# Routing pieces tied behind the one-hots, half-tile staging and fourteen leading up products, in a two-block transformer kernel

## The chip, the cores and the metric

The kernel runs on one core of a Trainium2 chip, as one launch. The metric is the device time of one execution in microseconds (us), as the median of repeated runs. The profile is of one execution; its times count from the first instruction of the span.

## The reference, cut to what matters

Two transformer blocks run over 512 tokens of width 1024, in float32. The change touches only the last layer of the second block, a mixture of 16384 tiny experts. For each token, `experts` are found as pairs of keys: eight heads, 16 pairs each, so 128 experts per token, each with a gate.

```python
def block(args):
    xb, eb, gb = args
    ub = u[eb]
    vb = v[eb]
    act = jax.nn.gelu(jnp.einsum('cd,ced->ce', xb, ub), approximate=False) * gb
    return jnp.einsum('ce,ced->cd', act, vb)
```

## The kernel before, in words

All large products run on TensorE (PE) as three fp32r products of split operands: `pump` loads a weight tile `w` (128x1024, 512 KB) by SyncE's DMA queue, ScalarE (ACT) rounds it to `wh`, and VectorE (DVE) or GpSimd (POOL) subtracts to get `wl`. The list `lsplit` says whose turn it is. Three slots each of `w`, `wh` and `wl` let loads run three tiles ahead of the splits, and splits three ahead of the products.

The expert layer (`peer`) treats tokens in four groups of 128. Group 0 gathers its experts' rows by indirect DMA. Groups 1 to 3 (384 tokens) work densely: for each of the 128 first keys j, `up(j)` multiplies the 384 tokens with 128 experts (24 matmuls of 384 columns, called one up product here), the result passes GELU, is multiplied by a gate matrix for j, and goes through the down product into six PSUM tiles. 42 of the 128 up products (`NA`) are made early: `up_store` writes their GELU to DRAM (`Hd`). They fill TensorE while the gate matrices are made, in the stage that this change is about:

- `route(t)` finds the 16 best pairs for each head of group t: eight `top16` searches, some twenty small operations on 128x128 tiles, and twice three operations on 128x2048 elements, all on VectorE, with one Exp on ScalarE. `transposed(t)` turns its three results by TensorE into the tile `rt`.
- `onehots(t, rt)` makes the gate matrices. It takes four tokens at a time, 32 times (a "quad", `q4`): `oh1` compares the first key with 0 to 127 (on POOL for a third of the quads, else on VectorE), `oh2` the second key, times the gate. A third of the quads scale `oh2` on ScalarE, the others make it by four VectorE instructions. Four fp32 matmuls of oh1 and oh2 (two records each in the trace) give 4x128x128 gates in PSUM, and ScalarE copies them into `stage`, two tiles that hold 64 of the columns j for all 128 tokens each. `fill(1)` places one up product after every fifth quad.
- For groups 1 and 2 both tiles then go to DRAM (`Gd`), in eight DMAs of 1 MB in rows of 512 bytes (the flush), with two up products after each pair. Group 3 stays in `stage`.

A scheduler orders the instructions of each engine ahead of time; on the chip every engine and every DMA queue then runs in that order. VectorE's tables of 0 to 127 and 0 to 15 lie in PSUM (`iotp`, `iotap`).

Of the kernel before, what the change touches and what calls it, by code (L numbers as in the profile page):

```python
# [43 lines left out]
def body(tc, A, out, upto=None, dbg=None):  # L44
# [13 lines left out]
    def mmps():  # L58
        return psum.tile([P, 512], F32, name="mm", tag="mm", bufs=4)
# [1094 lines left out]
    def peer(norm):  # L1154
# [95 lines left out]
                if ahead:  # L1250
                    up_store(ahead.popleft())

        def route(t):
            V.tensor_copy(tfp.rearrange("p (a b) -> p a b", b=16), ti[t])
            tf = tfp.rearrange("p (h f k) -> p h f k", f=2, k=16)


            bv = r_("bv", (P, 8, 16))
            bi = r_("bi", (P, 8, 16), dt=U32)
            cd = r_("cd", (P, 8, 60))  # L1260
            lists = tv[t].rearrange("p (h f) k -> p h f k", f=2)
            for i0, n, w, o in ((0, 1, 16, 0), (1, 2, 8, 16), (3, 5, 4, 32), (8, 8, 1, 52)):
                V.tensor_tensor(cd[:, :, o:o + n * w].rearrange("p h (i j) -> p h i j", j=w),
                                lists[:, :, 0, i0:i0 + n].rearrange("p h (i o) -> p h i o", o=1)
                                .to_broadcast([P, 8, n, w]),
                                lists[:, :, 1, 0:w].rearrange("p h (o j) -> p h o j", o=1)
                                .to_broadcast([P, 8, n, w]), ALU.add)
            for h in range(8):
                top16(bv[:, h], bi[:, h], cd[:, h])
            pf = r_("pf", (P, 8, 16))  # L1270
            V.tensor_copy(pf, bi)
            fi, fj, w_ = (r_(n, (P, 8, 16)) for n in ("fi", "fj", "fw"))
            for n, (sh, off) in enumerate(((3, -1.0), (2, -5.0))):
                pi = r_("pi", (P, 8, 16), dt=U32)
                V.tensor_scalar(pi, bi, sh, None, op0=ALU.logical_shift_right)
                V.tensor_copy(w_, pi)
                if n == 0:
                    V.tensor_scalar(fi, w_, off, 0.0, op0=ALU.add, op1=ALU.max)
                else:
                    V.scalar_tensor_tensor(fi, w_, off, fi, op0=ALU.add, op1=ALU.max)  # L1280
            V.scalar_tensor_tensor(fi, pf, -44.0, fi, op0=ALU.add, op1=ALU.max)
            V.scalar_tensor_tensor(fj, fi, -16.0, pf, op0=ALU.mult, op1=ALU.add)
            for m, off in ((-8.0, -8.0), (-4.0, -20.0), (-1.0, -44.0)):
                V.scalar_tensor_tensor(w_, fi, m, pf, op0=ALU.mult, op1=ALU.add)
                V.scalar_tensor_tensor(fj, w_, off, fj, op0=ALU.add, op1=ALU.max)
# [12 lines left out]
            gt = gate0 if t == 0 else r_("gt", (P, P), bufs=2)
# [7 lines left out]
            return ev[0], ev[1], gt  # L1306


        stp = rctx.enter_context(tc.tile_pool(name="st", bufs=1, side="right", reuse_waits="tile"))
        def transposed(t):  # L1310
            pt = axps()
            for n, a in enumerate(route(t)):
                PE.transpose(pt[:, n * P:(n + 1) * P], a, ident)
            rt = b_("rt", (P, 3, P), bufs=3)
            SC.activation(rt, pt[:, :3 * P].rearrange("p (n k) -> p n k", n=3), AF.Copy)
            return rt

        def onehots(t, rt):
            io4 = iotp.rearrange("p (o i) -> p o i", o=1).to_broadcast([P, 4, P])
            stage = [stp.tile([P, 64, P], F32, name="stage", tag="stage", bufs=2) for _ in range(2)]  # L1320
            for q4 in range(32):
                t4 = slice(4 * q4, 4 * q4 + 4)

                def cols(n):
                    return rt[:, n, t4].rearrange("p (t o) -> p t o", o=1).to_broadcast([P, 4, P])
                oh1 = b_("oh1", (P, 4, P), bufs=3)
                if q4 % 3 == 1:
                    for k in range(4):
                        G.tensor_scalar(oh1[:, k], iot, rt[:, 0, 4 * q4 + k:4 * q4 + k + 1], None, op0=ALU.is_equal)
                else:  # L1330
                    V.tensor_tensor(oh1, cols(0), io4, ALU.is_equal)
                oh2 = b_("oh2", (P, 4, P), bufs=3)
                on_act = q4 % 3 == 0
                if on_act:
                    V.tensor_tensor(oh2, cols(1), io4, ALU.is_equal)
                pg = axps()
                for k in range(4):
                    tk = 4 * q4 + k
                    if on_act:
                        SC.activation(oh2[:, k], oh2[:, k], AF.Copy, scale=rt[:, 2, tk:tk + 1])  # L1340
                    else:
                        V.tensor_scalar(oh2[:, k], iotp, rt[:, 1, tk:tk + 1], rt[:, 2, tk:tk + 1],  # L1342
                                        op0=ALU.is_equal, op1=ALU.mult)
                    PE.matmul(pg[:, k * P:(k + 1) * P], lhsT=oh1[:, k], rhs=oh2[:, k], start=True, stop=True)  # L1344
                for jh in range(2):
                    SC.activation(stage[jh][:, :, t4].rearrange("p j t -> p t j"),  # L1346
                                  pg.rearrange("p (t j) -> p t j", t=4)[:, :, jh * 64:jh * 64 + 64], AF.Copy)
                if q4 % 5 == 2:
                    fill(1)
            if t == 3:  # L1350
                return stage
            lsplit[:] = [V, G]
            for n in range(4):
                for j0 in (0, 16):
                    jj = 32 * (n % 2) + j0
                    nc.sync.dma_start(Gd[64 * (n // 2) + jj:64 * (n // 2) + jj + 16, :, (t - 1) * P:t * P]
                                      .rearrange("j i t -> i j t"), stage[n // 2][:, jj:jj + 16])
                fill(FLUSH[n])

        lsplit[:] = [V, G]  # L1360
        fill(FIRST)
        for t in (1, 2, 3):
            rt = transposed(t)
            lsplit[:] = [G]
            stage = onehots(t, rt)
        fill(NA)
        e1, e2, _ = route(0)
        V.scalar_tensor_tensor(e1, e1, 128.0, e2, op0=ALU.mult, op1=ALU.add)
        V.tensor_copy(idx, e1)
        lctx.close()  # L1370
# [84 lines left out]
            fetched[j] = gm, g  # L1455

        def gate(j):
            gm, st = fetched.pop(j)
            g = (mmps, axps)[turn[0] % 2]()[:, :TD]
            turn[0] += 1  # L1460
            if st is None:
                up(j, g)
                SC.activation(g, g, AF.Gelu)
            else:
                SC.activation(g, st, AF.Copy)
            V.tensor_tensor(g[:, :2 * P], g[:, :2 * P], gm, ALU.mult)
            V.tensor_tensor(g[:, 2 * P:], g[:, 2 * P:], stage[j // 64][:, j % 64], ALU.mult)
            a = hp.tile([P, TD], F32R, name="ah", tag="ah", bufs=3)
            b = hp.tile([P, TD], F32R, name="al", tag="al", bufs=3)
            SC.activation(a, g, AF.Copy)  # L1470
            last_dve[0] = V.tensor_tensor(b, g, a.bitcast(F32), ALU.subtract)  # L1471
            waiting.append((j, a, b))
# [219 lines left out]
```

## Time and profile before

| | us |
|---|---|
| median of three runs | 2961.1 (2959.9 to 2962.53) |
| the profiled execution, its own time | 2960.28 |
| its span, first to last instruction | 2957.9 |
| busy in the span: PE, DVE, ACT, POOL | 2900.9, 1929.8, 1376.7, 1158.4 |

The profiled execution lies 0.8 us below the median, and 2.4 us of its time lie outside the span. TensorE is busy for 98% of the span, VectorE for 65%. The one-hot stage begins with the first matmul on `xnh` at 1750.02 us and ends with the transposes of L1404 at 2054.66 us. A matmul's record is longer than its turn on the engine, since records overlap; a turn is read from starts that follow each other.

### The profile page before, as it was taken

The numbers are of one execution on the slowest core, as the hardware profiler recorded it, in microseconds if no ns is written. First come the engines' busy times: TensorE is split into PE (matmuls) and PEld (weight loads), VectorE is DVE, ScalarE is ACT, GpSimd is POOL, SyncE is SP. The second block draws the span as 40 slices with busy tenths as digits, with TensorE's granted clock in tenths as the row PEclk, the third lists the DMA queues.
The fourth block names the chain that finished last, engine by engine and source line by source line (L and its number), as shares of the span: only waits on it lengthen the run. The fifth ranks groups of instructions, "written<-read, shape, count | busy, mean of one in ns | idle before, by whom it ended". The sixth has DMA issues, their size and how long they took to land.

```text
span 2957.9 us, 46911 instructions
## 1 busy us (share of the span) xinstructions
PE 2900.9 (98%) x18211; PEld 2619.5 (89%) x18211; DVE 1929.8 (65%) x3505; ACT 1376.7 (47%) x2346; POOL 1158.4 (39%) x749
## 2 busy tenths in 40 slices
PE   8999999999999999999999999889999999999998
PEld 8999999988899999776688888888889888888887
DVE  4556645567664646537655788888677776776676
ACT  4454433356542425434544447567444444444444
POOL 4224323342232424104421435446455554555453
PEclk9999999999999999999999999999999999999999
DMA  4112333331123223221142232773888888888885
GB/s 136 67 52 101 98 96 101 97 104 36 65 97 97 96 98 110 85 72 52 49 150 66 86 111 79 226 225 113 304 330 311 312 317 316 330 307 302 308 315 188
DMA packets 166126, 473.41 MB, mean 160 GB/s; under 512 B 15368, under 2 KB 79240, under 8 KB 149520
## 3 DMA queue, kind: packets, MB, share of 16 engines
q1 hardware_dynamic: 135840, 322.73, 32.4%
q0 software_dynamic: 18432, 134.23, 11.8%
q10 hardware_dynamic: 11632, 13.46, 1.4%
q8 instruction: 143, 2.34, 0.3%
q14 instruction: 79, 0.65, 0.1%
HBM read 443.23 MB, written 27.13 MB: 159 GB/s over the span
## 4 chain that ended last, share of the span: by engine, by line
PE 89%; DVE 4%; ACT 3%; DMA 2%; issue 2%; POOL 1%; SPq 0%; ACTq 0%; DVEq 0%; POOLq 0%
PE mm L192 65%; PE ax L192 16%; PE ax L1344 2%; DMA w<-in_pu_dram 1%; ACT wh L115 1%; ACT stage L1346 1%; PE mm L1027 1%; PE ax L478 1%; PE ax L1207 1%; PE ax L997 0%; PE ax L453 0%; DVE wl L118 0%; DVE oh L1342 0%; PE mm L1021 0%; DMA xT<-in_xT_dram 0%
## 5 line engine op out<-in xcount | busy, mean ns | idle before, releaser
L118 POOL TENSOR_TENSOR wl<-w,wh 128x1024 fp32r<-128x1024 f32 x242 | 618.5, 2556 | 1058.2 <-ACT wh L115 893.7
L115 ACT ACTIVATE wh<-w 128x1024 fp32r<-128x1024 f32 (+1 forms) x530 | 560.0, 1057 | 854.1 <-PE mm L192 484.9
L192 PE MATMUL mm<-sh,wh 128*128 128x256 f32 (+2 forms) x3144 | 747.7, 303 | 7.0 <-ACT sh L225 6.2
L192 PE MATMUL mm<-sl,wh 128*128 128x256 f32 (+2 forms) x3144 | 744.6, 302 | 1.8 <-POOL sl L205 1.6
L192 PE MATMUL mm<-sh,wl 128*128 128x256 f32 (+2 forms) x3144 | 743.1, 301 | 1.0 <-DVE wl L118 1.0
L118 DVE TENSOR_TENSOR wl<-w,wh 128x1024 fp32r<-128x1024 f32 (+1 forms) x288 | 367.9, 1277 | 284.1 <-ACT wh L115 275.7
L192 PEld LDWEIGHTS mm<-sh,wh 128*128 128x128 f32 (+1 forms) x3144 | 498.9, 188 | 40.1 <-ACT sh L225 6.2
L192 PEld LDWEIGHTS mm<-sl,wh 128*128 128x128 f32 (+1 forms) x3144 | 497.9, 188 | 31.8 <-POOL sl L205 2.0
L192 PEld LDWEIGHTS mm<-sh,wl 128*128 128x128 f32 (+1 forms) x3144 | 497.9, 188 | 30.1 <-DVE wl L118 1.3
L192 PE MATMUL mm<-xnh,wl 128*128 128x384 f32 x688 | 237.1, 345 | 4.5 <-POOL wl L118 3.9
L192 PE MATMUL mm<-xnh,wh 128*128 128x384 f32 x688 | 237.5, 345 | 4.0 <-ACT wh L115 3.9
L192 PE MATMUL mm<-xnl,wh 128*128 128x384 f32 x688 | 236.8, 344 | 0.0
L285 DVE TENSOR_TENSOR xT<-xT,mm 128x512 f32<-128x512 f32 x80 | 54.7, 686 | 163.4 <-PE mm L192 163.4
L192 PE MATMUL mm<-wh,al 128*128 128x512 f32 x384 | 150.1, 391 | 2.5 <-DVE al L1471 2.5
L192 PE MATMUL mm<-wh,ah 128*128 128x512 f32 x384 | 150.3, 391 | 1.7 <-ACT ah L1470 1.7
L192 PE MATMUL mm<-wl,ah 128*128 128x512 f32 x384 | 150.2, 391 | 0.0
L192 PE MATMUL ax<-wh,ah 128*128 128x512 f32 x384 | 149.8, 390 | 0.0
L192 PE MATMUL ax<-wl,ah 128*128 128x512 f32 x384 | 149.7, 390 | 0.0
L192 PE MATMUL ax<-wh,al 128*128 128x512 f32 x384 | 149.4, 389 | 0.0
L561 POOL TENSOR_TENSOR y<-y 128x512 f32<-128x512 f32 x44 | 56.9, 1293 | 220.7 <-ACT y L560 220.7
L553 DVE SCALAR_TENSOR_TENSOR y<-u,vecs,y 128x512 f32<-128x512 f32 x88 | 113.9, 1295 | 44.5 <-ACT y L552 44.5
L192 PEld LDWEIGHTS mm<-xnh,wh 128*128 128x128 f32 x688 | 131.3, 191 | 6.4 <-ACT wh L115 4.6
(465 smaller groups left out, 5434.7 us busy)
## 6 DMA issues: line engine op xcount, KB each, us to landing
w<-in_pu_dram SPq DMA_DIRECT2D x128, 512.0 KB
w<-in_pv_dram SPq DMA_DIRECT2D x128, 512.0 KB
w<-in_up_dram SPq DMA_DIRECT2D x88, 512.0 KB
w<-in_down_dram SPq DMA_DIRECT2D x48, 512.0 KB
Gd<-stage SPq DMA_DIRECT2D x16, 1024.0 KB
gm<-Gd SPq DMA_DIRECT2D x128, 128.0 KB
w<-in_pq_dram SPq DMA_DIRECT2D x16, 512.0 KB
Hd<-gel ACTq DMA_DIRECT2D x42, 192.0 KB
```

The source lines that it names most:

```text
L115: SC.activation(h[:, :n], w[:, :n], AF.Copy)
L118: ins = eng.tensor_tensor(l[:, :n], w[:, :n], h[:, :n].bitcast(F32), ALU.subtract)
L192: PE.matmul(ps[:, c:c + w], lhsT=a, rhs=b[:, c:c + w], start=start and c == 0 and a is lh and b is rh, stop=stop and c + w == n and a is ll)
L285: V.tensor_tensor(xT[:, c], xT[:, c], ps, ALU.add)
L478: PE.matmul(ps[:, s], lhsT=a, rhs=b, start=i == 0, stop=i == len(mms) - 1)
L553: V.scalar_tensor_tensor(y, u[:, 0:S], w[0], y, op0=ALU.mult, op1=ALU.add)
L561: G.tensor_tensor(val, val, gate, ALU.mult)
L1027: PE.matmul(po[e * 64:e * 64 + 64, c * P:], lhsT=vs[:, c, hd * 64:hd * 64 + 64], rhs=at[:, c * P:], start=c == 0, stop=c == 3)
L1207: PE.matmul(pss[:, t * P:(t + 1) * P], lhsT=q[:, t * P:(t + 1) * P], rhs=sk, start=True, stop=True)
L1344: PE.matmul(pg[:, k * P:(k + 1) * P], lhsT=oh1[:, k], rhs=oh2[:, k], start=True, stop=True)
L1346: SC.activation(stage[jh][:, :, t4].rearrange("p j t -> p t j"), pg.rearrange("p (t j) -> p t j", t=4)[:, :, jh * 64:jh * 64 + 64], AF.Copy)
```

## The change

The routing of the next group no longer stands between two groups. `route` becomes a generator that stops after each piece; `onehots(t, rt, nxt)` runs the next group's pieces behind its own quads, where `issue_after` ties each piece on VectorE behind the instruction `own` of that quad. The yielded costs set how many pieces follow a quad. `oh2` is now scaled on ScalarE for every second quad; the other quads make it by two VectorE instructions on 128x512 elements, by way of a PSUM tile of the pool that the up products use. A stage tile now holds all 128 columns for 64 tokens; one ScalarE copy of 128x512 takes the place of two of 128x256, and each half is flushed when its 16 quads are done, in eight DMAs of 512 KB in rows of 256 bytes. Fourteen up products in place of six stand ahead of the first routing, two follow every seven quads, none stands with the flush, and all weight splits of the stage are POOL's. In the later stage each gate multiply reads two 64-column pieces of `stage` in place of one of 128.

```diff
-FIRST, FLUSH = 6, (2, 2, 2, 2)
+FIRST = 14
...
-        def route(t):
+        def route(t, out):
...
+            yield 1.5
             for h in range(8):
                 top16(bv[:, h], bi[:, h], cd[:, h])
+                yield 1.3
...
-        def onehots(t, rt):
+        def onehots(t, rt, nxt):
...
-            stage = [stp.tile([P, 64, P], F32, name="stage", tag="stage", bufs=2) for _ in range(2)]
+            res, spent, nrt = [], 0.0, None
+            steps = route(nxt, res)
+            stage = []
             for q4 in range(32):
+                if q4 % 16 == 0:
+                    st = stp.tile([P, P, 64], F32, name="stage", tag="stage", bufs=2)
+                    stage.append(st)
...
-                on_act = q4 % 3 == 0
-                if on_act:
-                    V.tensor_tensor(oh2, cols(1), io4, ALU.is_equal)
+                if q4 % 2 == 0:
+                    own = V.tensor_tensor(oh2, cols(1), io4, ALU.is_equal)
+                    for k in range(4):
+                        SC.activation(oh2[:, k], oh2[:, k], AF.Copy, scale=rt[:, 2, 4 * q4 + k:4 * q4 + k + 1])
+                else:
+                    eq = mmps().rearrange("p (t j) -> p t j", t=4)
+                    V.tensor_tensor(eq, cols(1), io4, ALU.is_equal)
+                    own = V.tensor_tensor(oh2, eq, cols(2), ALU.mult)
...
-                        V.tensor_scalar(oh2[:, k], iotp, rt[:, 1, tk:tk + 1], rt[:, 2, tk:tk + 1],
-                                        op0=ALU.is_equal, op1=ALU.mult)
...
+                SC.activation(st[:, :, o:o + 4].rearrange("p j t -> p t j"),
+                              pg.rearrange("p (t j) -> p t j", t=4), AF.Copy)
+                while spent < 1.45 * (q4 + 1) and steps is not None:
+                    with tc.issue_after(own.ins):
+                        c = next(steps, None)
...
-                if q4 % 5 == 2:
+                if q4 % 7 in (2, 5):
                     fill(1)
-            lsplit[:] = [V, G]
-            for n in range(4):
...
-                fill(FLUSH[n])
+                if q4 % 16 == 15 and t < 3:
+                    c0 = (t - 1) * P + (q4 // 16) * 64
+                    for j0 in range(0, P, 16):
+                        nc.sync.dma_start(Gd[j0:j0 + 16, :, c0:c0 + 64].rearrange("j i t -> i j t"),
+                                          st[:, j0:j0 + 16])
...
-        lsplit[:] = [V, G]
+        lsplit[:] = [G]
         fill(FIRST)
...
-            V.tensor_tensor(g[:, 2 * P:], g[:, 2 * P:], stage[j // 64][:, j % 64], ALU.mult)
+            for n, st in enumerate(stage):
+                c = slice(2 * P + n * 64, 2 * P + n * 64 + 64)
+                V.tensor_tensor(g[:, c], g[:, c], st[:, j], ALU.mult)
```

On VectorE, before the change, the routing of group 2 runs in one stretch between the one-hots of groups 1 and 2 (L1284 and L1285 are small steps, L1290, L1293 and L1296 the wide ones, L118 a weight split):

```order
L1290 TENSOR_TENSOR oh<-fi,ax 128x2048
L1285 SCALAR_TENSOR_TENSOR fj<-fw,fj 128x128
L1293 TENSOR_TENSOR oh<-oh,ax 128x2048
L118 TENSOR_TENSOR wl<-w,wh 128x1024
L1284 SCALAR_TENSOR_TENSOR fw<-fi,pf 128x128
L1296 TENSOR_REDUCE e_19175<-oh 128x128
```

On VectorE with the change, at the same steps of that routing (now L1295, L1288, L1289, L1299 and L1303), one-hots of group 1 stand between (L1346 is `oh1`, L1349 the compare of an even quad, L1354 and L1355 the two instructions of an odd one):

```order
L1295 TENSOR_TENSOR oh<-fi,ax 128x2048
L1289 SCALAR_TENSOR_TENSOR fj<-fw,fj 128x128
L1346 TENSOR_TENSOR oh_18738<-rt,ax 128x512
L1288 SCALAR_TENSOR_TENSOR fw<-fi,pf 128x128
L1349 TENSOR_TENSOR oh_18740<-rt,ax 128x512
L1289 SCALAR_TENSOR_TENSOR fj<-fw,fj 128x128
L1354 TENSOR_TENSOR mm<-rt,ax 128x512
L1288 SCALAR_TENSOR_TENSOR fw<-fi,pf 128x128
L1355 TENSOR_TENSOR oh_18791<-mm,rt 128x512
L1289 SCALAR_TENSOR_TENSOR fj<-fw,fj 128x128
L1299 TENSOR_TENSOR oh<-oh,ax 128x2048
```

The routing pieces moved between the one-hots, and the weight split left VectorE; the last routing piece of a group stands at quad 22 or 23 of 32, and only one-hots follow.

On SyncE's DMA queue, before the change, weight loads (L110) stand between the pairs of the flush (L1356):

```order
L1356 DMA Gd<-stage 128x16x128 x2
L110 DMA w<-in_pu_dram 128x1024
L1356 DMA Gd<-stage 128x16x128 x2
L110 DMA w<-in_pu_dram 128x1024 x2
L1356 DMA Gd<-stage 128x16x128 x2
L110 DMA w<-in_pu_dram 128x1024 x2
L1356 DMA Gd<-stage 128x16x128 x2
L110 DMA w<-in_pu_dram 128x1024 x9
```

On the same queue with the change, each half tile's flush (L1376) is one block of eight, in both groups:

```order
L110 DMA w<-in_pu_dram 128x1024 x16
L1376 DMA Gd<-stage 128x16x64 x8
L110 DMA w<-in_pu_dram 128x1024 x4
L1376 DMA Gd<-stage 128x16x64 x8
L110 DMA w<-in_pu_dram 128x1024 x5
L1376 DMA Gd<-stage 128x16x64 x8
L110 DMA w<-in_pu_dram 128x1024 x4
L1376 DMA Gd<-stage 128x16x64 x8
L110 DMA w<-in_pu_dram 128x1024 x3
```

The flush moved from two places to four, and the weight loads stand behind whole blocks of eight. In ScalarE's order the rounding of that weight stands 11 or 12 quads after the copy that starts the flush.

## Rows read from the trace of the kernel before

**Rows 1.** Windows: busy us per engine, granted clock, DMA share, GB/s.
```profile
core 0: us, PE busy (x) PEld busy (x) DVE busy (x) ACT busy (x) POOL busy (x), PEclk, DMA share, GB/s
1750.00:2055.00 305.00, 281.56 (x1799) 270.44 (x1798) 263.98 (x775) 205.24 (x428) 154.03 (x163) 0.96 0.50 157
1776.00:1792.00 16.00, 10.12 (x51) 9.92 (x50) 15.30 (x30) 2.98 (x5) 4.76 (x2) 0.79 0.27 102
1792.00:1850.00 58.00, 56.81 (x406) 54.21 (x404) 48.30 (x118) 51.31 (x119) 37.53 (x49) 1.00 0.20 67
1850.00:1890.00 40.00, 34.15 (x179) 32.65 (x178) 34.05 (x106) 14.23 (x23) 8.33 (x8) 0.87 1.03 307
2075.00:2945.00 870.00, 868.26 (x4296) 776.43 (x4295) 627.50 (x871) 382.81 (x729) 453.42 (x228) 1.00 0.83 305
```

**Rows 2.** Waits of PE, 1750 to 2055 us: total, times, longest.
```profile
PE ax L1344 <- ACT oh L1340: 7.6, 10, 4.3
PE ax L1313 <- DVE e L1296: 5.9, 1, 5.9
```

**Rows 3.** The chain that ended last, in order of time: start, us, what.
```profile
1799.63 1.90 PE ax L1344 x16
2049.97 4.69 PE mm L192 x27
2054.66 0.87 PE ax L1404 x8
```

**Rows 4.** Timeline of PE: start, us, engine, line, operation.
```profile
1750.02 0.33 PE L192 MATMUL mm<-xnh,wh 128*128 128x384 f32 x1
...
1791.59 0.27 PE L1313 MATMUL ax<-ident,gt 128*128 128x128 f32 x1
...
1794.25 2.05 PE L1344 MATMUL ax<-oh,oh 128*128 128x128 f32 x16
```

**Rows 5.** Timeline of DVE, 1757 to 1800 us.
```profile
1758.15 0.41 DVE L1254 CAST ax<-ti 128x256 f32<-128x256 uint32 x1
...
1759.60 0.35 DVE L1185 MAX8 bv<-cd 128x8 f32<-128x60 f32 x2
...
1762.30 1.21 DVE L118 TENSOR_TENSOR wl<-w,wh 128x1024 fp32r<-128x1024 f32 x1
...
1767.40 0.27 DVE L1300 TENSOR_TENSOR gt<-bv 128x128 f32<-128x128 f32 x1
...
1773.63 2.50 DVE L1285 SCALAR_TENSOR_TENSOR fj<-fw,fj 128x128 f32<-128x128 f32 x1
1776.05 2.27 DVE L1293 TENSOR_TENSOR oh<-oh,ax 128x2048 f32<-128x2048 f32 x1
...
1781.85 0.28 DVE L1285 SCALAR_TENSOR_TENSOR fj<-fw,fj 128x128 f32<-128x128 f32 x1
...
1792.42 0.69 DVE L1331 TENSOR_TENSOR oh<-rt,ax 128x512 f32<-128x512 f32 x1 [1.12 <-ACT rt L1315]
1793.02 0.68 DVE L1335 TENSOR_TENSOR oh<-rt,ax 128x512 f32<-128x512 f32 x1
1793.62 1.36 DVE L1342 TENSOR_SCALAR oh<-ax,rt 128x128 f32<-128x128 f32 x4
1794.90 0.68 DVE L1331 TENSOR_TENSOR oh<-rt,ax 128x512 f32<-128x512 f32 x1
```

**Rows 6.** Timeline of POOL, 1772 to 1784 us.
```profile
1773.03 2.95 POOL L118 TENSOR_TENSOR wl<-w,wh 128x1024 fp32r<-128x1024 f32 x1 [5.91 <-ACT wh L115]
```

**Rows 7.** Timeline of ACT, 1811 to 1850 us.
```profile
1812.61 2.92 ACT L1346 ACTIVATE stage<-ax 128x256 f32<-128x256 f32 x6 [0.40 <-PE ax L1344]
1815.33 1.24 ACT L1340 ACTIVATE oh<-oh,rt 128x128 f32<-128x128 f32 x4
```

**Rows 8.** Groups by line and shape, 1750 to 2055 us: count, busy, mean ns, idle before.
```profile
L118 POOL TENSOR_TENSOR wl<-w,wh 128x1024 fp32r<-128x1024 f32 x31 | 74.6, 2407 | 109.7 <-ACT wh L115 106.1 <-DVE pi L1275 3.6
L115 ACT ACTIVATE wh<-w 128x1024 fp32r<-128x1024 f32 x43 | 45.5, 1059 | 57.7 <-PE mm L192 29.1 <-DMA w<-in_pu_dram 18.3 <-DVE bi L1186 6.1
```

**Rows 9.** DMA queue q1 (packets, MB, share): 1876 to 1881, then 1555 to 1560 us.
```profile
q1 hardware_dynamic: 3242, 1.66, 109.8%
...
q1 hardware_dynamic: 144, 0.52, 32.0%
```

More of the change, by code (lines that the diff above doesn't have):

```diff
@@ L1280, in route @@
                     V.scalar_tensor_tensor(fi, w_, off, fi, op0=ALU.add, op1=ALU.max)
+            yield 2.0
             V.scalar_tensor_tensor(fi, pf, -44.0, fi, op0=ALU.add, op1=ALU.max)
@@ L1285, in route @@
                 V.scalar_tensor_tensor(fj, w_, off, fj, op0=ALU.add, op1=ALU.max)
+            yield 3.0
             ev = []
@@ L1291, in route @@
                                 iotap.rearrange("p (o i) -> p o i", o=1).to_broadcast([P, P, 16]), ALU.is_equal)
+                yield 2.3
                 o4 = oh.rearrange("p (h k) i -> p h k i", k=16)
@@ L1294, in route @@
                                 .to_broadcast([P, 8, 16, 16]), ALU.mult)
+                yield 2.3
                 e = r_(f"e{half}", (P, P), bufs=2)
@@ L1297, in route @@
                 ev.append(e)
+                yield 2.3
             gt = gate0 if t == 0 else r_("gt", (P, P), bufs=2)
@@ L1305, in route, with transposed @@
             V.tensor_tensor(g3, g3, sm.rearrange("p (h o) -> p h o", o=1).to_broadcast([P, 8, 16]), ALU.mult)
-            return ev[0], ev[1], gt
+            out.extend((ev[0], ev[1], gt))
+            yield 2.0
         stp = rctx.enter_context(tc.tile_pool(name="st", bufs=1, side="right", reuse_waits="tile"))
-        def transposed(t):
+        def transposed(res):
             pt = axps()
-            for n, a in enumerate(route(t)):
+            for n, a in enumerate(res):
                 PE.transpose(pt[:, n * P:(n + 1) * P], a, ident)
-            rt = b_("rt", (P, 3, P), bufs=3)
+            rt = b_("rt", (P, 3, P), bufs=2)
             SC.activation(rt, pt[:, :3 * P].rearrange("p (n k) -> p n k", n=3), AF.Copy)
             return rt
-        def onehots(t, rt):
+        def onehots(t, rt, nxt):
             io4 = iotp.rearrange("p (o i) -> p o i", o=1).to_broadcast([P, 4, P])
-            stage = [stp.tile([P, 64, P], F32, name="stage", tag="stage", bufs=2) for _ in range(2)]
+            res, spent, nrt = [], 0.0, None
+            steps = route(nxt, res)
+            stage = []
             for q4 in range(32):
+                if q4 % 16 == 0:
+                    st = stp.tile([P, P, 64], F32, name="stage", tag="stage", bufs=2)
+                    stage.append(st)
                 t4 = slice(4 * q4, 4 * q4 + 4)
@@ L1336, in onehots @@
                 pg = axps()
                 for k in range(4):
-                    tk = 4 * q4 + k
-                    if on_act:
-                        SC.activation(oh2[:, k], oh2[:, k], AF.Copy, scale=rt[:, 2, tk:tk + 1])
-                    else:
-                        V.tensor_scalar(oh2[:, k], iotp, rt[:, 1, tk:tk + 1], rt[:, 2, tk:tk + 1],
-                                        op0=ALU.is_equal, op1=ALU.mult)
-                    PE.matmul(pg[:, k * P:(k + 1) * P], lhsT=oh1[:, k], rhs=oh2[:, k], start=True, stop=True)
@@ L1345, in onehots @@
-                for jh in range(2):
-                    SC.activation(stage[jh][:, :, t4].rearrange("p j t -> p t j"),
-                                  pg.rearrange("p (t j) -> p t j", t=4)[:, :, jh * 64:jh * 64 + 64], AF.Copy)
-                if q4 % 5 == 2:
-                    fill(1)
-            if t == 3:
-                return stage
-            lsplit[:] = [V, G]
-            for n in range(4):
[L1354 to L1357, printed above, removed]
-                fill(FLUSH[n])
@@ L1360, in peer @@
-        lsplit[:] = [V, G]
+                    PE.matmul(pg[:, k * P:(k + 1) * P], lhsT=oh1[:, k], rhs=oh2[:, k], start=True, stop=True)
+                o = 4 * (q4 % 16)
+                SC.activation(st[:, :, o:o + 4].rearrange("p j t -> p t j"),
[3 more added lines that the diff above has]
+                        c = next(steps, None)
+                    if c is None:
+                        steps = None
+                    else:
+                        spent += c
@@ new lines, in onehots @@
+                if steps is None and nrt is None:
+                    nrt = transposed(res) if nxt else res
+                if q4 % 7 in (2, 5):
+                    fill(1)
+                if q4 % 16 == 15 and t < 3:
[3 more added lines that the diff above has]
+                                          st[:, j0:j0 + 16])
+            if steps is not None:
+                for _ in steps:
+                    pass
+                nrt = transposed(res) if nxt else res
@@ L1361, in peer @@
+            return stage, nrt
+        lsplit[:] = [G]
         fill(FIRST)
+        res = []
+        for _ in route(1, res):
+            pass
+        rt = transposed(res)
         for t in (1, 2, 3):
-            rt = transposed(t)
-            lsplit[:] = [G]
-            stage = onehots(t, rt)
+            stage, rt = onehots(t, rt, (t + 1) % 4)
         fill(NA)
-        e1, e2, _ = route(0)
+        e1, e2, _ = rt
         V.scalar_tensor_tensor(e1, e1, 128.0, e2, op0=ALU.mult, op1=ALU.add)
@@ L1457, in gate @@
         def gate(j):
-            gm, st = fetched.pop(j)
+            gm, gs = fetched.pop(j)
             g = (mmps, axps)[turn[0] % 2]()[:, :TD]
             turn[0] += 1
-            if st is None:
+            if gs is None:
                 up(j, g)
@@ L1464, in gate @@
             else:
-                SC.activation(g, st, AF.Copy)
+                SC.activation(g, gs, AF.Copy)
             V.tensor_tensor(g[:, :2 * P], g[:, :2 * P], gm, ALU.mult)
-            V.tensor_tensor(g[:, 2 * P:], g[:, 2 * P:], stage[j // 64][:, j % 64], ALU.mult)
+            for n, st in enumerate(stage):
+                c = slice(2 * P + n * 64, 2 * P + n * 64 + 64)
+                V.tensor_tensor(g[:, c], g[:, c], st[:, j], ALU.mult)
             a = hp.tile([P, TD], F32R, name="ah", tag="ah", bufs=3)
```

## The prediction

> **What bounds the kernel now.** I read the windows first. From 2075 to 2945 us PE is busy for 868 of 870 us [rows 1]: nothing but PE's own work counts there, and the change adds none. The one-hot stage is looser: from 1750 to 2055 PE is busy for 281.6 of 305 us, at a granted clock of 0.96. The chain of waits says what a full PE would need. 27 up matmuls take 4.69 us, so an up product of 24 takes 4.17 us, and 16 records of one-hot matmuls take 1.90 us, 0.119 each [rows 3]. 42 up products and 768 records make 175.1 + 91.4 us; with 1 us for nine transposes, 267.5 us. The stage takes 304.6, from 1750.0 to 2054.7 [rows 3, 4]. So 37 us are at stake: 23.4 idle, the rest lost at the lower clock.
>
> The reader is to see where they lie. While one-hots run (1792 to 1850) PE is busy for 56.8 of 58 us at clock 1.00; ACT and DVE have 51.3 and 48.3 there. PE waits where routing stands alone: 5.9 us in one piece for the first routing [rows 2], in a window whose clock is 0.79; and during the flush (1850 to 1890), PE idles for 5.9 us of 40 at clock 0.87, while the DMA share is 1.03 [rows 1]. ACT waited 18.3 us in the stage for weights behind the flush [rows 8]. The change goes for just these two places, and pays by making DVE and ACT work harder during one-hots.
>
> **The start.** Fourteen up products take 58.4 us, to 1808.4. The first routing runs on DVE meanwhile. Its parts: cast and sums, 1758.15 to 1759.60, 1.45 us; eight searches to 1767.40, 7.8 less the split at 1762.30 (1.1), 6.7; some nineteen small steps of about 0.17, 3.2; six wide ones of 2.2 (a 2.27 record, less the 0.07 by which records overlap), 13.2. Sum 24.5 us [rows 5]. It ends by about 1786 even with every weight split on POOL in its way, 22 us ahead of PE. The first wait goes. What is late next: from the transposes to the first one-hot matmul PE has nothing to do but wait for rt, DVE and ACT. Before, 1791.59 to 1794.25 [rows 4], 2.7 us, covered by up matmuls; now uncovered. First quad: 1811.1. DVE stands idle for those 22 us and more, since its next instruction needs rt.
>
> POOL takes 2.41 us per split [rows 8], under the 4.17 of an up product, so giving it all of them costs nothing while loads come.
>
> **A group of 32 quads, engine by engine.** PE: 32 x 8 x 0.119 + 9 up products = 30.5 + 37.5 = 68.0 us.
>
> DVE: a 128x512 instruction takes a turn of 0.60, four 128x128 scalings 1.28 (1793.62 to 1794.90) [rows 5]. oh1 in 21 quads 12.6, compares of 16 even quads 9.6, two instructions of 16 odd quads 19.2: 41.4, or 1.3 per quad (before: 12.6 + 6.6 + 26.9 = 46.1). The PSUM round trip of the odd quads is not in the trace; bounds are 0.53 (a 128x512 turn without a fixed part, by the slope of the 2048 ones, 2.2/4) and 0.69 (the whole record) each; I keep 0.60, nearest in shape. Added is the next routing, 24.5.
>
> One more term is DVE against POOL. At 1773.63 a 128x128 step that takes 0.28 at 1781.85 took 2.50, and it ended when POOL's split (1773.03, 2.95 us) did [rows 5, 6]. Its operands all lie in SBUF; one-hots, with a PSUM operand, show no such rows. About two such hits per routing, 2.7 us, is what the four routings before averaged; small steps now stand apart, each with its own chance of a hit, but POOL splits for only 9 x 2.4 = 22 of some 70 us. I take 2.7, bounds 0 and 9. DVE in all: 68.6.
>
> ACT: a copy of 128x256 takes a turn of (2.92 - 0.64)/5 = 0.456; a scaling (1.24 - 0.39)/3 = 0.283 [rows 7]. The 128x512 copy with its 256-byte steps is not in the trace: at least 0.66 (one record of the old copy), at most twice the old turn, 0.91; I take 0.9, since time went by elements. 32 x 0.9 + 64 x 0.283 + nine roundings of 1.06 [rows 8] + some 9 for GELUs, tables and rt = 66.
>
> So three engines have 66 to 69 us each, and the order decides. Routing pieces end by quad 23. Up to there DVE has 23 x 1.3 + 24.5 + 2.7 = 57.1 us, PE only 23 x 0.95 + 6 x 4.17 = 47: DVE sets the pace. In the last nine quads PE has 9 x 0.95 + 3 x 4.17 = 21.1, DVE 11.7: PE sets it, and DVE runs ahead into the next group by its three buffers and the first sums, about 5 us. 57.1 + 21.1 - 5 = 73.2 per group; three make 219.6. All pieces that wait behind a tied one are one-hots, which is already in the 57.1.
>
> **The flush.** Its cover was the eight up products; now it is one-hots and up products at a slower draw: nine in 73 us. A block of eight moves 4.19 MB as 16384 packets of 256 bytes over 16 engines, 1024 each. A 512-byte packet takes 109.8% x 16 x 5000/3242 = 27.1 ns, a 4 KB one 32.0% x 16 x 5000/128 = 200 ns (the 16 others are tiny) [rows 9]. So time goes nearly by bytes; the line through both gives 14.8 ns at 256 bytes, the bounds are 13.6 (half) and 27.1 (no saving), and with some slack I take 17: 17.4 us per block. The load behind it is wanted by ACT 11 or 12 quads later, 11 x 2.5 = 27 us. So it is hidden with some 8 us to spare, and costs nothing; at 27.1 ns the block takes 27.8 us, and load and block together (30) overrun by 3 us, 12 for the four blocks.
> The Trainium skill's page "DMA: Bandwidth & Descriptors", section Specifications, speaks against this: it asks for at least 512 bytes per transfer, since below that the engine does read-modify-write. No write under 512 bytes shows in this trace. By that rule the blocks would not be hidden, and the sum would be 2985 (second rival); by the rows they are, and it is 2945.
>
> **The later stage.** 128 more VectorE instructions of some 0.2 us, 25 us, where DVE has 627 of 870 us busy [rows 1]; products wait two gates deep. Hidden; if none of it were, 128 x 0.2 = 25 us, which is unlikely at 72% load.
>
> **The sum.** 1811.1 + 219.6 + one last up product 4.2 = 2034.9, against 2054.7: -19.8 us. DVE sets PE's pace for 57 us of each group, in short gaps; where PE idled for 5.9 us its clock fell [rows 1, 2], so I add 4 us for spells at the low clock. -16 from the profiled 2960.3, so 2944; the median lies 0.8 higher: **2945 us**.
>
> **Rivals.**
> First, better: buffers smooth DVE's and PE's turns, and a group takes PE's 68 us. 3 x 5.2 less, without the clock's 4: 2925. For it: before, one-hots ran at 98% PE with ACT at 88%. Against: DVE's first 23 quads can't shrink.
> Second, slower: the 256-byte flush. Place: the rounding on ACT behind which one-hot scalings queue, as in the 18.3 us before. If a packet is read and written back, two turns of 17, 34 ns: 34.8 us a block, with the load 37; 10 over the 27, four times: +40, 2985. It decides above +22, i.e. at 5.5 us over, a block of 30.5 us or 30 ns a packet. The Trainium skill's page "DMA: Bandwidth & Descriptors" would have it so.
> Third, no change: groups of 78 to 79 us. DVE/POOL hits at their bound (+6 in a group), or PE at half clock while DVE sets the pace, give back the 16 us: 2960.
> Fourth, worse than that: shared PSUM tiles (the odd quads' eq waits for a GELU that ACT holds back behind copies), 3 us more in each group on top of the third: 2970.
>
> **How the numbers follow.** Forecast 0.58 (own range 2932 to 2957), first rival 0.12, second 0.13, third 0.12, fourth 0.05. 0.2% of 2961 is 6 us, about what a measurement of this kernel can tell from no change. Faster by more: 0.53 of the forecast, and the first rival, 0.65, and a little of the third, 0.67. Slower: second and fourth, 0.17. The rest, 0.16, is the same. The range leaves out the best of the first rival and the worst of the second: 2924 to 2972.
>
> **What would show it.** PE's first one-hot matmul near 1811 and no wait for L1303 before it; groups of some 73 us by the starts of quad 0; PE's waits in a group's first two thirds, for oh2; no rounding on ACT that waits for a weight DMA; a packet of 256 bytes at 15 to 20 ns. A DMA share near 1 for over 25 us after a flush, or a rounding that waits for its load, shows the second rival; small VectorE steps of over 1 us, more than three per group, or a clock under 0.9, the third.

## The result, and the profile after

The changed kernel takes 2974.2 us (median of nine, 2969.2 to 2988.6), the kernel before 2960.6 beside it (nine, 2957.9 to 2963.4): a ratio of 1.0053, interval 1.0038 to 1.0068. It is 13.6 us slower, where I forecast 16 faster; that lies outside my range of 2932 to 2957, and 2 us above the wider one that ends at 2972. The profiled execution took 2972.67 us, its span is 2971.0, 13.1 more than before.

The windows of the changed kernel, to be read beside [rows 1]:
```profile
core 0: us, PE busy (x) PEld busy (x) DVE busy (x) ACT busy (x) POOL busy (x), PEclk, DMA share, GB/s
1750.00:2060.00 310.00, 279.91 (x1797) 268.31 (x1796) 247.24 (x624) 223.67 (x392) 177.88 (x174) 0.99 0.58 156
1775.00:1791.00 16.00, 16.00 (x95) 16.00 (x94) 15.93 (x12) 5.76 (x8) 9.14 (x4) 1.00 0.57 181
1812.42:1895.33 82.91, 72.86 (x475) 68.93 (x476) 72.82 (x185) 64.96 (x119) 47.46 (x56) 0.98 0.48 127
1895.33:1974.72 79.39, 71.01 (x477) 67.39 (x476) 69.37 (x163) 65.44 (x119) 47.10 (x53) 1.00 0.77 189
1974.72:2055.44 80.72, 72.32 (x475) 68.78 (x474) 64.26 (x140) 64.09 (x115) 44.66 (x49) 0.98 0.52 138
2075.00:2945.00 870.00, 867.91 (x4262) 771.09 (x4262) 661.68 (x983) 380.33 (x710) 422.84 (x231) 1.00 0.85 307
```
The three windows in the middle are the three groups: each begins at its first one-hot matmul (768 records, 256 to a group), and the third ends with its last. The clock is mended: 0.99 in the stage, against 0.96. PE is full while the first routing runs. But in groups of 82.9, 79.4 and 80.7 us PE is busy for 71 to 73, DVE for 64 to 73, ACT for 64 to 65: no engine is full, and PE idles 8 to 10 us in each. In the down stage DVE has 34 us more to do than before, and PE's records there are still nearly gapless.

What PE waited for from 1750 to 2060 us (total, times, longest), beside [rows 2]:
```profile
PE ax L1358 <- ACT oh L1351: 27.6, 29, 3.3
PE ax L1358 <- DVE oh L1355: 1.7, 3, 0.9
```
The wait for the first routing (5.9) is gone; waits for the scaled one-hots rose from 7.6 us to 27.6.

Landmarks of PE's timeline, beside [rows 4]: the transposes of the first routing, the first one-hot matmul, the transposes that end the stage, the first down matmul:
```profile
1808.88 0.27 PE L1322 MATMUL ax<-ident,gt 128*128 128x128 f32 x1
...
1812.42 1.14 PE L1358 MATMUL ax<-oh,oh 128*128 128x128 f32 x4 [3.26 <-ACT oh L1351]
...
2059.44 1.04 PE L1430 MATMUL ax<-ident,xT 128*128 128x128 f32 x8
...
2073.71 0.79 PE L192 MATMUL mm<-wh,ah 128*128 128x512 f32 x1 [3.71 <-ACT ah L1498]
```
I compare all kernels by such landmarks. The time before the first up matmul is left out: the change doesn't touch it, and it varies between executions (1746.4 to 1765.4 us in these profiles, as the kernel before itself goes from 2957.2 to 2977.5 us beside these runs). Each landmark is from one execution; kernels that share the code of the stage agree in it within 0.5 us (304.5, 304.2 and 304.0; 310.1 and 310.1). A ratio is to the kernel before as it ran beside that kernel. Two of the twelve executions of e4_act_third, of 5203 and 13433 us at clocks of 0.74 and 0.20, are not in its ratio. All in us; "stage" runs from the first up matmul to the end-of-stage transposes, "between" from there to the first down matmul, "down" from that to the end of PE's last matmul.

| kernel | first one-hot | stage | between | down | median | ratio, 95% |
|---|---|---|---|---|---|---|
| before | 44.2 | 304.5 | 12.5 | 884.3 | 2960.6 | |
| changed | 63.1 | 310.1 | 14.3 | 891.0 | 2974.2 | 1.0053 [1.0038, 1.0068] |
| e1_split_read | 44.1 | 304.2 | 14.7 | 889.4 | 2969.8 | 1.0031 [1.0013, 1.0048] |
| e2_one_tile | 63.0 | 310.1 | 15.1 | 883.5 | 2967.6 | 1.0016 [0.9998, 1.0034] |
| e3_four_bufs | 63.1 | 307.0 | 13.5 | 890.3 | 2968.4 | 1.0028 [1.0015, 1.0041] |
| e4_act_third | 63.0 | 312.5 | 13.5 | 891.6 | 2976.2 | 1.0046 [1.0028, 1.0064] |
| e5_even | 63.0 | 301.4 | 15.5 | 889.7 | 2966.7 | 1.0013 [0.9995, 1.0032] |
| e6_more_up | 46.4 | 297.1 | 13.5 | 890.5 | 2958.4 | 0.9976 [0.9958, 0.9994] |
| e7_joined | 46.4 | 281.3 | 13.3 | 883.1 | 2935.9 | 0.9907 [0.9878, 0.9936] |
| e8_four_reads | 44.1 | 304.0 | 15.0 | 916.3 | 2991.5 | 1.0101 [1.0085, 1.0118] |
| e9_act_two_thirds | 63.0 | 310.3 | 13.5 | 887.1 | 2970.3 | 1.0039 [1.0026, 1.0051] |
| e10_no_routing | 63.0 | 289.4 | 13.5 | 887.4 | 2948.0 | one run, 2958.6 before |

So the change costs 5.6 us in the stage, 1.8 between and 6.7 in the down stage.

The same stage by groups, in us, with the mean granted clock of each group; e2_one_tile has the changed kernel's three times:

| kernel | group 1 | group 2 | group 3 |
|---|---|---|---|
| changed | 82.9 (0.98) | 79.4 (1.00) | 80.7 (0.98) |
| e3_four_bufs | 82.5 (0.98) | 78.8 (1.00) | 78.7 (1.00) |
| e4_act_third | 85.2 (0.90) | 82.7 (0.92) | 77.6 (0.98) |
| e9_act_two_thirds | 84.9 (0.94) | 79.9 (0.98) | 78.5 (1.00) |
| e10_no_routing | 69.9 (0.98) | 69.3 (1.00) | 83.0 (0.98) |
| e5_even | 81.7 (0.94) | 76.6 (1.00) | 76.0 (1.00) |
| e6_more_up | 91.8 (0.93) | 82.0 (1.00) | 77.1 (1.00) |
| e7_joined | 80.9 (0.98) | 79.3 (1.00) | 74.8 (1.00) |

Where the second group goes, in DVE's timeline of the changed kernel:
```profile
1788.78 2.29 DVE L1303 TENSOR_REDUCE e<-oh 128x128 f32<-128x2048 f32 x1
1810.59 0.69 DVE L1346 TENSOR_TENSOR oh<-rt,ax 128x512 f32<-128x512 f32 x1 [19.52 <-ACT rt L1324]
...
1890.25 0.28 DVE L1264 TENSOR_TENSOR cd<-tv 128x128 f32<-128x128 f32 x1
...
1918.62 2.27 DVE L1295 TENSOR_TENSOR oh<-fi,ax 128x2048 f32<-128x2048 f32 x1
...
1946.28 0.39 DVE L1308 TENSOR_TENSOR gt<-bv 128x128 f32<-128x128 f32 x1
1946.59 0.67 DVE L1349 TENSOR_TENSOR oh<-rt,ax 128x512 f32<-128x512 f32 x1
1949.17 0.69 DVE L1346 TENSOR_TENSOR oh<-rt,ax 128x512 f32<-128x512 f32 x1 [1.91 <-PE ax L1358]
...
1964.03 0.69 DVE L1346 TENSOR_TENSOR oh<-rt,ax 128x512 f32<-128x512 f32 x1 [3.12 <-PE ax L1358]
...
1969.62 0.29 DVE L1264 TENSOR_TENSOR cd<-tv 128x128 f32<-128x128 f32 x1
```
The second group's pieces begin at 1890.25 (L1264). DVE runs with only 1.5 us of waits until 1947.26, 22 quads on; then it waits for PE's matmuls to free one-hot buffers, and the third group's pieces begin at 1969.62. The two stretches as windows:
```profile
1890.25:1947.26 57.01, 50.99 (x338) 48.49 (x338) 54.95 (x139) 43.38 (x82) 34.91 (x42) 1.00 0.76 185
1947.26:1969.62 22.36, 20.03 (x137) 18.91 (x137) 14.41 (x26) 22.04 (x40) 12.18 (x13) 1.00 0.78 197
```
In the first, of 57.0 us, DVE is busy for 55.0, ACT for 43.4: DVE sets it. In the second, of 22.4 us, DVE has slack, PE is busy for 20.0 and ACT for 22.0: PE and ACT set it between them, and ACT is the fuller. Together 79.4.

The flush, by DMA queue (packets, MB, share) from 1862 to 1867 us:
```profile
q1 hardware_dynamic: 4225, 1.07, 106.4%
```
That is 106.4% x 16 x 5000 / 4225 = 20.1 ns per packet of 256 bytes, beside 27.1 for 512 [rows 9].

ScalarE's groups of 1750 to 2060 us, beside [rows 8]:
```profile
L1360 ACT ACTIVATE stage<-ax 128x512 f32<-128x512 f32 x96 | 100.5, 1102 | 25.1 <-PE ax L1358 24.6
...
L115 ACT ACTIVATE wh<-w 128x1024 fp32r<-128x1024 f32 x42 | 44.4, 1057 | 45.9 <-PE mm L192 37.9 <-issue 4.8 <-POOL oh L1344 2.3
```
No rounding waits for a weight load any more (18.3 us before).

### The profile page after: what moved, and what is told of

It is laid out like the page before. It is cut to its first block, busy times and chain, and to the rows that moved or that the text cites. A ratio compares the mean times of both kernels' runs of the same rounds, so it can differ in the third digit from the quotient of the medians.

```text
span 2971.0 us, 46819 instructions
## 1 busy us (share of the span) xinstructions
PE 2905.9 (98%) x18211; PEld 2617.8 (88%) x18211; DVE 1953.8 (66%) x3481; ACT 1400.7 (47%) x2311; POOL 1146.0 (39%) x760
## 4 chain that ended last, share of the span: by engine, by line
PE 88%; ACT 5%; DVE 3%; issue 2%; DMA 1%; POOL 1%; ACTq 0%; DVEq 0%; SPq 0%; POOLq 0%
PE mm L192 66%; PE ax L192 15%; PE ax L1358 2%; ACT stage L1360 1%; ACT wh L115 1%; PE mm L1027 1%; PE ax L1207 1%; ACT oh L1351 0%; PE ax L478 0%; PE ax L997 0%; PE ax L453 0%; ACT gel L1243 0%; DVE xt L1464 0%; DMA scr<-in_ffn_norm_row_dram 0%; PE mm L1021 0%
## 5 line engine op out<-in xcount | busy, mean ns | idle before, releaser
L118 POOL TENSOR_TENSOR wl<-w,wh 128x1024 fp32r<-128x1024 f32 x253 | 628.5, 2484 | 1026.1 <-ACT wh L115 958.9
L192 PEld LDWEIGHTS mm<-sh,wl 128*128 128x128 f32 (+1 forms) x3144 | 498.4, 188 | 29.1 <-issue 1.1
L118 DVE TENSOR_TENSOR wl<-w,wh 128x1024 fp32r<-128x1024 f32 (+1 forms) x277 | 351.7, 1270 | 253.0 <-ACT wh L115 247.5
L1358 PE MATMUL ax<-oh,oh 128*128 128x128 f32 x768 | 110.5, 286 | 30.1 <-ACT oh L1351 27.6
```

The lines of the kernel that those rows point to most:

```text
L118: ins = eng.tensor_tensor(l[:, :n], w[:, :n], h[:, :n].bitcast(F32), ALU.subtract)
L192: PE.matmul(ps[:, c:c + w], lhsT=a, rhs=b[:, c:c + w], start=start and c == 0 and a is lh and b is rh, stop=stop and c + w == n and a is ll)
```

## The experiments

Two questions: why a group takes some 80 us, and why the down stage is longer.

**e1_split_read**: the kernel before, with this alone.
```diff
-            V.tensor_tensor(g[:, 2 * P:], g[:, 2 * P:], stage[j // 64][:, j % 64], ALU.mult)
+            for n in range(2):
+                c = slice(2 * P + n * 64, 2 * P + n * 64 + 64)
+                V.tensor_tensor(g[:, c], g[:, c], stage[j // 64][:, j % 64, n * 64:n * 64 + 64], ALU.mult)
```


> The kernel before, with the last group's 128 columns read by two multiplies of 64 instead of one of 128, and nothing else. Theory (the down stage pays for 128 more VectorE instructions): the stage end stays at 2054.5 us and the down stage is 5 to 8 us longer, so 2966 to 2968 us, with more scatter between runs. Rival (the forecast's own word, hidden behind the down products): 2960 to 2961 us.


Down stage 889.4 us, 5.1 more than before; the one-hot stage is unchanged (304.2). The split read alone gives most of the changed kernel's 6.7. Besides, the time between the stages is 2.2 us longer.

**e2_one_tile**: the changed kernel, with the two half tiles as one.
```diff
+        both = stp.tile([P, 2, P, 64], F32, name="stage", tag="stage", bufs=1)
...
-                    st = stp.tile([P, P, 64], F32, name="stage", tag="stage", bufs=2)
+                    st = both[:, q4 // 16]
...
-            for n, st in enumerate(stage):
-                c = slice(2 * P + n * 64, 2 * P + n * 64 + 64)
-                V.tensor_tensor(g[:, c], g[:, c], st[:, j], ALU.mult)
+            g2 = g[:, 2 * P:].rearrange("p (n t) -> p n t", n=2)
+            V.tensor_tensor(g2, g2, both[:, :, j], ALU.mult)
```


> The changed kernel, with both half tiles of a group in one tile of 2x128x64, so that the last group is read by one multiply of 2x64 columns; the one-hot stage and its flush are as changed. Theory (the second multiply costs the down stage its 6.7 us): stage end stays near 2059, down stage back to that of before, 2966 to 2968 us. Rival (the down stage's loss comes from where its work starts, not from the multiplies): 2973 to 2975 us.


Down stage 883.5: 7.5 less, with the stage at the same 310.1. Done and undone, the second multiply is the cause of the down stage's loss. The first gates scatter by 2 to 3 us between kernels, but this does not carry the finding: from the fifth gate to the end of PE's last matmul the kernel before, e2_one_tile and e7_joined take 861.4, 861.4 and 861.3 us, and the kernels with two reads 866.7 to 868.5.

What it does there is seen in DVE's groups from 2100 to 2900 us (count, busy, mean ns), first the kernel before:
```profile
L1429 DVE SCALAR_TENSOR_TENSOR scr<-uv,xn 128x1024 f32<-128x1024 f32 x60 | 91.4, 1523 | 0.6 <-DMA uv<-in_uv_dram,idx 0.6
L1438 DVE SCALAR_TENSOR_TENSOR xt<-uv,dot,xt 128x1024 f32<-128x1024 f32 x60 | 78.7, 1312 | 0.0
```
Then e1_split_read:
```profile
L1438 DVE SCALAR_TENSOR_TENSOR xt<-uv,dot,xt 128x1024 f32<-128x1024 f32 x59 | 103.8, 1760 | 0.0
...
L1429 DVE SCALAR_TENSOR_TENSOR scr<-uv,xn 128x1024 f32<-128x1024 f32 x60 | 74.5, 1242 | 0.0
```
And e2_one_tile:
```profile
L1457 DVE SCALAR_TENSOR_TENSOR scr<-uv,xn 128x1024 f32<-128x1024 f32 x60 | 91.4, 1523 | 0.0
...
L1466 DVE SCALAR_TENSOR_TENSOR xt<-uv,dot,xt 128x1024 f32<-128x1024 f32 x59 | 75.3, 1276 | 0.0
```
The mean of the first sum (dot) falls by 0.28 us and that of the second (combine) rises by 0.45: the slow ones are now the combines, which stand right ahead of the next gate. Of some 120 combines in this stretch, 2 take over 2.5 us in the kernel before, 29 in e1_split_read, 28 in the changed kernel and 1 in e2_one_tile; no other takes more than 1.28. One such place in the changed kernel, on DVE, then POOL, then PE:
```profile
2307.38 3.42 DVE L1464 SCALAR_TENSOR_TENSOR xt<-xT,dot,xt 128x1024 f32<-128x1024 f32 x1
2310.72 0.42 DVE L1492 TENSOR_TENSOR ax<-ax,gm 128x256 f32<-128x256 f32 x1
2311.18 0.50 DVE L1495 TENSOR_TENSOR ax<-ax,stage 128x64 f32<-128x64 f32 x2
2311.59 1.22 DVE L118 TENSOR_TENSOR wl<-w,wh 128x1024 fp32r<-128x1024 f32 x1
2312.72 0.42 DVE L1492 TENSOR_TENSOR mm<-mm,gm 128x256 f32<-128x256 f32 x1
2313.18 0.50 DVE L1495 TENSOR_TENSOR mm<-mm,stage 128x64 f32<-128x64 f32 x2
```
```profile
2306.76 2.95 POOL L118 TENSOR_TENSOR wl<-w,wh 128x1024 fp32r<-128x1024 f32 x1 [2.86 <-ACT wh L115]
```
```profile
2314.32 0.79 PE L192 MATMUL mm<-wh,ah 128*128 128x512 f32 x1 [2.09 <-ACT ah L1498]
```
The combine starts while POOL splits and ends 1.1 us after POOL does; two gates follow one behind the other, and PE waits 2.09 us for the second. It is the largest: the changed kernel loses 2.9 us there, and most of the rest in steps of some 0.4 us along the stage.

**e8_four_reads**: the kernel before, the loop of e1_split_read with four reads of 32 columns.
```diff
-            for n in range(2):
-                c = slice(2 * P + n * 64, 2 * P + n * 64 + 64)
+            for n in range(4):
+                c = slice(2 * P + n * 32, 2 * P + n * 32 + 32)
```


> The kernel before, with the last group's 128 columns read by four multiplies of 32. With two the down stage took 889.4 us, with one 884.3. Theory (VectorE's chain of a gate is late now and then, the later the longer it is): four multiplies of 0.20 instead of two of 0.23 put 0.3 us more on each gate's chain, and the down stage takes 892 to 900 us. Rival (the loss comes from the place where VectorE meets POOL's splits, a matter of phase and not of length): 884 to 890 us, no longer than with two.


Down stage 916.3 us, +32.0 for three more multiplies where the first had cost 5.1. The direction is that of length, the size beyond what I expected. PE's waits of that kernel from 2100 to 2940 us:
```profile
PE mm L192 <- ACT ah L1472: 23.1, 21, 3.5
```
In the same stretch it is one wait of 0.7 us before. I read this as a threshold: the gate's chain is near PE's pace before, and goes past it soon, with DVE busy for only 650 of 800 us. But 38 of 115 combines are slow there (29 of 119 in e1_split_read), so the meeting with POOL has its part too, and this run does not separate the two.

**e3_four_bufs**: the changed kernel with `bufs=4` for `oh1` and `oh2`.


> The changed kernel with four buffers instead of three for each of the two one-hots. Theory (three engines of 62 to 71 us each hold one another through the three buffers, so that a group takes 79.4): one more buffer takes 2 to 5 us off each group, 2958 to 2968 us. Rival (one engine's order sets the group and buffers don't matter): 2973 to 2975 us.


Stage 307.0, 1.0 us less per group on average (0.4, 0.6 and 2.0): the sign of the theory, under its size. A fourth buffer does little of what makes a group some 80 us.

**e4_act_third** and **e9_act_two_thirds**: the changed kernel, `q4 % 2 == 0` replaced by `q4 % 3 == 0` (11 quads scaled on ACT) and by `q4 % 3 != 1` (21).


> The changed kernel with ScalarE's scalings for every third quad (11 of 32) instead of every second (16): ScalarE has 5 x 4 x 0.39 = 7.8 us less per group, VectorE 5 x 0.60 = 3.0 more. Theory (TensorE waits for scalings that stand late in ScalarE's order): groups of 75 to 77 us, 2960 to 2968 us. Rival (VectorE's sum sets the group): groups of 82 us, 2981 to 2985 us.

> The changed kernel with ScalarE's scalings for 21 of 32 quads instead of 16: VectorE has 5 x 0.60 = 3.0 us less per group, ScalarE 5 x 4 x 0.28 = 5.7 more; the mirror of the run with 11. Theory (VectorE's work in the first 23 quads sets a group's middle): stage end 2 to 6 us earlier than the changed kernel's 310.1 us after the first up product, 304 to 308. Rival (TensorE waits for ScalarE's scalings, which come later still): 312 to 320 us.


Stage 312.5 and 310.3 against 310.1. Neither of the two bands of either run holds it, and these sums hide what happened. (The 7.8 us in the first text counts ScalarE's records of 0.39; by turns of 0.28 it is 5.7, as in the second.) With 21 quads on ACT, the second group's stretch from the first routing piece to the last is 52.5 us instead of 56.0, as the theory has it; but the stretch behind it is 27.5 instead of 23.3, and ACT is busy for 25.5 of it. What DVE gains, ACT gives back. With 11 quads on ACT the first two groups are 2.3 and 3.3 us longer, near the rival's, but at clocks of 0.90 and 0.92; the third, at the changed kernel's clock of 0.98, is 3.1 shorter, at 77.6 near the theory's 75 to 77. So this run does not separate DVE's added work, ACT's lesser work and the clock; what each is worth stays open.

**e10_no_routing**: the second and third routing left out.
```diff
-            steps = route(nxt, res)
+            steps = None if nxt else route(nxt, res)
...
-                    nrt = transposed(res) if nxt else res
+                    nrt = rt if nxt else res
```


> The changed kernel without the routing of the second and third group (they use the lists of the first; so the routing of these tokens is left out, with its two transposes and table loads); the last group still carries the routing pieces of the first tokens. Theory (routing pieces on VectorE make a group's middle late): the first two groups take 70 to 73 us each instead of 79.4, with no wait of TensorE over 1 us in them, and the third stays at 78 to 80. Rival (ScalarE's scalings and copies set the group, with or without pieces): 77 to 80 us for each.


The stage is 20.7 us shorter: the two groups without pieces are 13.0 and 10.1 us shorter, the third 2.3 longer. Its windows of the three groups:
```profile
1812.78:1882.70 69.92, 68.72 (x469) 67.05 (x470) 43.91 (x71) 59.59 (x115) 45.98 (x56) 0.98 0.55 144
1882.70:1952.03 69.33, 67.86 (x474) 66.16 (x473) 46.02 (x90) 59.91 (x115) 44.42 (x53) 1.00 0.86 208
1952.03:2035.08 83.05, 72.39 (x475) 68.52 (x474) 66.34 (x140) 64.88 (x116) 48.08 (x51) 0.98 0.54 147
```
With the same scalings, copies and up products, 98% of a group is PE's, at the same clocks as in the changed kernel, and 82.9 and 79.4 us become 69.9 and 69.3; the third, which has pieces and is the first to have them, takes 83.0, as the first does in the changed kernel. ACT is busy for 60 of those 69 us, so it does not bound a group without pieces. The pieces on DVE (some 26 us in each of the two groups) cost 10 to 13 of them. The run took away a little on ACT and PE as well, two table loads, one exp, one copy and three transposes per group, some 4 us beside the 26.

**e5_even**: the changed kernel with the pieces handed out at 1.2 per quad instead of 1.45.


> The changed kernel with the routing pieces handed out at 1.2 per quad instead of 1.45, so that they end by quad 27 or 28 instead of 23. Theory (in the middle of a group VectorE has one-hots and wide routing pieces one behind the other, PE waits there, and cannot make it up in the last nine quads): 1 to 3 us less per group, 2966 to 2972 us. Rival (three buffers bind ScalarE, TensorE and VectorE everywhere alike, whatever the order): 2973 to 2975 us.


Stage 301.4, 2.9 us less per group on average (1.2, 2.8 and 4.7): as the theory has it. In the second group the pieces now take 62.0 us from the first to the last instead of 56.0, and leave 14.9 behind them instead of 23.3: the same work is spread wider, and DVE and PE work side by side for longer.

**e6_more_up**: four fewer up products ahead, two more in a group.
```diff
-FIRST = 14
+FIRST = 10
...
-                if q4 % 7 in (2, 5):
+                if q4 % 3 == 1:
```


> The changed kernel with ten up products instead of fourteen ahead of the one-hots, and eleven (after every third quad) instead of nine in a group. Theory (a group lasts 79.4 us for VectorE's sake in its middle, with 8 us of TensorE idle, so up products there cost little): the first one-hot matmul 16.7 us earlier, near 1796; groups of 80 to 83 us instead of 79.4; stage end 2040 to 2048 against 2059.4; 2957 to 2965 us. Rival (groups are the sum of what each engine hands to the next, so each up product adds its 4.2 us): groups of 87 to 88 us, stage end near 2060, 2973 to 2978 us.


The one-hots begin 16.7 us earlier, and 32 up products follow their start instead of 28: 11, 11 and 10 in the groups and none behind, against 9 in each and one behind. From the first one-hot to the stage's end it is 250.7 us, against 247.0, so four more up products of 4.17 us cost 3.7 together. They don't cost it evenly: the first group, at a clock of 0.93, takes 91.8 us, the 87 to 88 of the rival and more; the second, at 1.00, pays 2.6 for its two more; the third is 3.6 shorter than the changed kernel's. The stage takes 297.1, and the kernel is a little faster than the one before.

**e7_joined**: the edits of e2, e3, e5 and e6 together.


> The changed kernel with four edits together: half tiles in one tile read by one multiply, four buffers for the one-hots, pieces at 1.2 per quad, ten up products ahead and eleven in a group. If the edits add up (down stage -7 us, buffers -3, pieces -3 to -6, up products -12 to -20): stage end 2030 to 2040, down stage as before, 2940 to 2950 us, below the kernel before. Rival (they all recover the same idle time of TensorE, so that only the largest counts, beside the down stage): 2952 to 2958 us.


Stage 281.3: 28.8 less than the changed kernel, where the parts alone gave 3.1, 8.7 and 13.0, so they add up and a little more. Its first group ran at a clock of 0.98, where e5_even and e6_more_up had 0.94 and 0.93, which may be the little more. Down stage 883.1. 2935.9 us, ratio 0.9907 (0.9878 to 0.9936): below both kernels. Its windows, the stage and the down stage:
```profile
1746.00:2031.00 285.00, 273.92 (x1826) 268.19 (x1825) 250.43 (x633) 221.22 (x395) 179.69 (x174) 0.99 0.64 173
2061.00:2931.00 870.00, 861.36 (x4254) 769.11 (x4252) 623.72 (x870) 381.48 (x732) 450.21 (x227) 1.00 0.82 302
```

## Why the prediction was wrong

**The start: right.** First one-hot matmul at 1812.4, forecast 1811.1; PE full until 1808.7, no wait for the routing. The routing ended at 1791.1, not 1786, still 17 us ahead.

**A group: wrong, at one step of its sum.** The loads stood: PE's 68.0 us came out as 68 to 69 in groups without pieces and 71 to 73 with them, DVE's 68.6 as 64 to 73, ACT's 66 as 64 to 65. So did the turn of 0.60, and the hits between DVE and POOL: by the means of L1281, L1286, L1288 and L1289 (1.06, 0.81, 0.43 and 0.71 us instead of 0.28) some 12 us over four routings, 3.0 each, where I had 2.7. "DVE sets the pace" for 57.1 us measured 57.0. "PE sets it" for 21.1 measured 22.4, and ACT, which I had left out there, was fuller than PE. What failed is the third term: "DVE runs ahead into the next group by its three buffers and the first sums, about 5 us". DVE does run ahead by 5.1 us: the third group's pieces begin at 1969.62, its one-hot matmuls at 1974.72. But it was ahead by as much when the group began (1890.25 and 1895.33), so the lead moves both ends of the period and shortens none. Without it the sum is 78.2, measured 79.4.

Three times 5 is 15 of the 24.5 us by which the stage's end was missed (2059.4, forecast 2034.9). Another 1.2 per group is 3.6; the first group takes 3.5 more than the second, since it begins without a lead (pieces at 1811.79, first matmul at 1812.42) and with its clock at 0.98; the third takes 1.3 more, also at 0.98; the first quad is 1.3, and the last up product 0.2 less than forecast. e10_no_routing and e5_even show the mechanism from both sides: without the pieces a group is PE's 69 us, with them thinner it is 2.9 shorter.

**The later stage: wrong.** "Hidden": it cost 6.7 us, shown by e1_split_read, e2_one_tile and, with more reads still, e8_four_reads. I reasoned from DVE's load of 72%. That slow combines ahead of a gate are the way is read from rows; no run moved POOL's splits alone.

**The clock: small.** I added 4 us for spells at the low clock. In the groups it was 0.98, 1.00 and 0.98, which can have cost some 3 us at most, 2% of the first and the third.

**Between the stages** 1.8 us were not in the sum. With the old one-hot stage and split reads it is 14.7 and 15.0, with the new stage and one read 15.1 and 13.3, with both 13.5 to 15.5: no part of the change is singled out, and it stays open. Together: 24.5 - 4 + 1.8 + 6.7 = 29.0, against 13.1 + 16 = 29.1 us of error in the span.

**The rivals.** First (68 us per group): its bound is real, and e10_no_routing's groups without pieces show it, 69 us; e7_joined has 96% PE in the stage by other edits. Second (flush): refuted. A packet took 20.1 ns, above my 17 and under the 30 from which it decides; a block of 1024 packets per engine is then 20.6 us, under the 27 of its cover, and no rounding waited for its load. Of the read-modify-write that the Trainium skill's page "DMA: Bandwidth & Descriptors", section Specifications, names below 512 bytes, no added cost of a packet shows here: 20.1 ns for 256 bytes against 27.1 for 512. By byte the smaller packet does cost more, 20.1 against 13.6 for half of the larger. Third (groups of 78 to 79 us): near in its number (79.4 to 82.9), wrong in its causes, hits and clock; its 2960 then lacked the down stage. Fourth (PSUM tiles): DVE's write of that tile (L1354) never waited, and the second instruction of an odd quad 1.4 us in all three groups, so no.

## What to carry to other kernels

Where a round has a stretch that one engine sets and a stretch that another sets, the round takes the sum of the two: a lead through buffers is paid back each round, and is no gain. What helped here was to mix the stretches, by thinning the late engine's work over the whole round and by moving work of the idle engine into the stretch where it waits.
When two runs differ in a stage, read the clock of each group beside its time, and don't take a third of a stage for a group: sums of three hid opposite signs in e4_act_third and e9_act_two_thirds.
An engine that is busy for 72% of a stage is no cover if what it makes is due at each step: count its longest chain between two due times, not its load.

## What the runs showed of the hardware that I had not expected

One multiply of 128x2x64 does what two of 128x64 do in less time: 0.30 us in e2_one_tile, as one of 128x128 takes, against 2 x 0.23 as two.
A VectorE sum of 128x1024 with all operands in SBUF, 1.28 us as a rule, took 3.42 when a GpSimd split had begun 0.6 us before it: it ended 1.1 us after the split (2309.71). This is no single case: in the kernel before, from 2100 to 2900 us, 60 such sums began while a split of weights ran on POOL, and every one ended 1.08 or 1.09 us after that split; the 180 others took 1.21 to 1.28.
Stores in packets of 256 bytes ran at 215 GB/s, 20.1 ns each, in the 5 us shown above.
